# Retention slabs split from the unsplit tile, and the window groups' sample rows computed in the retention stage

## The chip, the cores and the metric

One core of one Trainium2 chip runs the kernel. The metric is the device time of one execution in microseconds (us); lower is better. A run is repeated and the median is given. The engines are TensorE (PE, with PEld for its weight loads), VectorE (DVE), ScalarE (ACT), GpSimd (POOL) and SyncE (SP), which here issues nearly all transfers (DMAs).

## The reference

One layer of a hybrid decoder for 1024 prompt tokens and 8 sample tokens (one token each of 8 requests), all in float32, model width 1024:

```
h = rms_norm(x) * g
[ret q|k|v|gate, swa q|k|v|gate, merge gates] = h @ w_in
A: retention, 4 heads (q, k of 128, v of 256), chunks of 128 tokens, state kept; sample rows: one step on a given state
B: sliding-window attention (128), 4 groups of 4 query heads and one key/value head of 64, sinks, rotary;
   sample rows: one query each against a cache of 128 rows, whose last row is the new key/value
y = x + (sigmoid(mr) * (gated A @ w_ret) + sigmoid(ms) * (gated B @ w_swa)) @ w_out
```

The outputs are y of prompt and samples, the retention states and the window caches.

## The kernel before, in words

A float32 operand is held as two parts, hi (rounded to PE's faster float32 form) and lo (the rest), and each product is three matmuls: hi·hi, hi·lo and lo·hi. Weights come from memory in *units*. A unit is loaded by SP into a raw tile `wraw` (3 buffers), ACT writes its hi part `whi` (L167) and POOL its lo part `wlo` (L168); 6 buffers of each. A T unit is 128 columns of w_in over all 8 blocks of 128 rows and feeds `gemm_T` (L211 to L213): 24 matmuls for one block of 344 of the 1032 tokens. A K unit (*slab*) is 2 of the 8 row blocks of a group's 384 columns; four slabs feed `gemm_tok` (L221 to L223): 24 matmuls for one tile of 128 tokens.

The first phase begins with the startup: 9 token tiles x0 to x8 (x8 holds the 8 sample rows) are loaded, normed (`norm_h`; DVE's product is L281, its 1/root comes from POOL, L146), transposed on PE (L286) and split into `hhi` and `hlo` (L138, L139). For x8 two more forms are stored: `hx`, its plain float32 transposed, and `hs`, with the hi rows at columns 0 to 7 and the lo rows at 32 to 39 of 40 (L290, L292). Then come four retention groups (gi 0 to 3, one head each) and four window groups (gi 4 to 7). A group works through 8 token tiles; between them stand T blocks: gates, merge gates, and the retention q, whose rotation is three operations on DVE (L325 to L327).

The sample rows of a group are computed apart. In a retention group `quad_rows` (L249) takes the *unsplit* weights: the group's 384 columns are loaded a second time, whole, into `rraw` (L241), and 8 matmuls with the 8 columns of `hx` go to four column tiles of PE; one ACT copy and three DVE additions (L250, L252) sum the four. In a window group `gemm_rows` (L231, L232) takes the split weights that the group has anyway: 16 matmuls of `hs` with `whi` and `wlo`, an ACT copy (L235) and a DVE addition (L236). Then the rows get their rotation, the new key is stored in the cache tile `cK`, which POOL copies to `kc` (L617) for PE's transposes (L620).

A second phase does the branch projections and the output. The program is put in order by the framework's scheduler (L1029), which decides what stands before what on every engine, so a change in one place can move instructions in another. SP and each engine take their list in order: an instruction that waits holds up what stands behind it.

Of the kernel before, what the change touches and what calls it, by code (L numbers as in the profile page):

```python
# [9 lines left out]
F32 = mybir.dt.float32  # L10
F32R = mybir.dt.float32r
# [7 lines left out]
P = 128  # L19
# [26 lines left out]

MROW = 40
MLO = 32
KST = 64 + NS
# [7 lines left out]
QAT = (1, 2, 4)  # L57
ROW = [2, 0, 0, 0, 2, 0, 0, 1]
FILL = [3, 2, 2, 2, 9, 9, 9, 4]
# [62 lines left out]
class Body:  # L122
# [27 lines left out]
    def load_unit(self, spec):  # L150
        nc = self.nc
        kind, segs, k0, nk = spec
        width = sum(w for _, _, w in segs)
        raw = self.t(self.wp, [P, D], "wraw", bufs=RAW)
        hi = self.t(self.wp, [P, D], "whi", F32R, bufs=self.wbufs)
# [69 lines left out]

    def gemm_rows(self, ps, units, st, out, n):
        nc = self.nc
        k = 0
        for whi, wlo in units:
            for kk in range(whi.shape[1]):  # L230
                nc.tensor.matmul(ps, st[:, k, :], whi[:, kk, :], start=(k == 0), stop=False)  # L231
                nc.tensor.matmul(ps, st[:, k, :], wlo[:, kk, :], start=False, stop=(k == KT - 1))  # L232
                k += 1
        tmp = self.t(self.sm, [NS, 512], "rowtmp", bufs=1)
        nc.scalar.activation(out=tmp[:, :n], in_=ps[MLO : MLO + NS, :n], func=AF.Copy)  # L235
        nc.vector.tensor_tensor(out=out, in0=ps[:NS, :n], in1=tmp[:, :n], op=ALU.add)  # L236

    def load_rows(self, tile, segs):
# [16 lines left out]
    def norm_h(self, t):  # L255
# [26 lines left out]
        for half in range(2):  # L282
            ps = self.t(self.ptr, [P, 4, P], "tr")
            for j in range(4):
                k = half * 4 + j
                nc.tensor.transpose(out=ps[:, j, :p], in_=x[:p, k * P : (k + 1) * P], identity=self.ident[:p, :p])  # L286
            ks = slice(half * 4, half * 4 + 4)
            self.copy_hi_lo(self.hhi[:, ks, cs], self.hlo[:, ks, cs], ps[:, :, :p], nc.vector)
            if t == NT:
                nc.scalar.activation(out=self.hs[:, ks, 0:NS], in_=ps[:, :, :p], func=AF.Copy)  # L290
                nc.vector.tensor_copy(out=self.hx[:, ks, :], in_=ps[:, :, :p])
                nc.vector.tensor_copy(out=self.hs[:, ks, MLO : MLO + NS], in_=self.hlo[:, ks, cs].bitcast(F32))  # L292

# [297 lines left out]
    def swa_rows(self, g, units, oT):  # L591
        nc = self.nc
        gs = slice(g * HD, (g + 1) * HD)
        K, V = self.cK[:, :, gs], self.cV[:, :, gs]
        acc = self.t(self.pacc, [P, 512], "acc")
        kv = self.t(self.ap, [NS, 384], "rkv", bufs=1)
        self.gemm_rows(acc[:MROW, :384], units, self.hs, kv[:], 384)
        qr, kd, rs = self.swa_rope(kv[:], NT, NS)
# [78 lines left out]
    def build(self):  # L677
# [4 lines left out]
        with tc.tile_pool(name="const", bufs=1, reuse_waits="tile") as cp, tc.tile_pool(name="sm", bufs=2, reuse_waits="tile") as sm, \  # L682
# [6 lines left out]
            self.d_o = [self.t(dp, [P, TOK], f"d_o{k}") for k in range(16)]  # L689
            self.d_t = [self.t(dp, [P, TOK], f"d_t{k}") for k in range(16)]  # L690
            self.d_m = [self.t(dp, [P, TOK], f"d_m{k}") for k in range(8)]
            self.misc = self.t(cp, [P, NMISC], "misc")
# [9 lines left out]
    def phase1(self):  # L702
        nc, tc = self.nc, self.tc
        with tc.tile_pool(name="h", bufs=1, reuse_waits="tile") as hp:
            self.hhi = self.t(hp, [P, KT, TOK], "hhi", F32R)
            self.hlo = self.t(hp, [P, KT, TOK], "hlo", F32R)
            self.hs = self.t(hp, [P, KT, MROW], "hs", F32R)
            self.hx = self.t(hp, [P, KT, NS], "hx")
            nc.vector.memset(self.hs[:].bitcast(F32), 0.0)
            self.hT = [(self.hhi[:, k, :], self.hlo[:, k, :]) for k in range(KT)]  # L710
# [6 lines left out]
    def groups(self):  # L717
        nc = self.nc
        tch = lambda c: ("T", (("w_in", c, P),), 0, KT)

        def slabs(cols):
            return [("K", tuple(("w_in", c, w) for c, w in cols), 2 * j, 2) for j in range(4)]

# [26 lines left out]

        kv = slabs([(OFF_RK, DK), (OFF_RV, DV)])
        qu = tch(OFF_RQ)
# [27 lines left out]
        def tables(us):  # L780
# [6 lines left out]
        steps += [([], begin, 0), x(0), w(kv[0]), x(1), w(kv[1]), x(2), w(kv[2]), w(kv[3]), ([], tables, 0), x(3), w(qu),  # L787
                  x(4), x(5), rope_block(0), x(6), x(7), x(8), rope_block(1), rope_block(2)]
        prev = []
        pipe = []  # L790
# [5 lines left out]
        for gi in range(8):  # L796
# [5 lines left out]
            if ret:  # L802
                h = gi

                def setup(us, h=h, st=st):
                    st["o"] = self.t(self.gp, [P, 2, TOK], "oT", bufs=2)
                    st["q"] = self.t(self.ap, [P, TOK], "qT", bufs=2)
                    st["S"] = self.t(self.ap, [P, DV], "S", bufs=2)
                    self.rraw = self.t(self.ap, [P, KT, 384], "rraw", bufs=1)
                    self.load_rows(self.rraw, [("w_in", OFF_RK + h * DK, DK), ("w_in", OFF_RV + h * DV, DV)])  # L810
                put(([], setup))
                qs = [([tch(OFF_RQ + h * DK)], lambda us, st=st, nb=nb: self.ret_q(us[0], st["q"], nb)) for nb in range(NB)]
                if h:
                    put(*qs)
                kv = slabs([(OFF_RK + h * DK, DK), (OFF_RV + h * DV, DV)])
                mk = lambda u, t, h=h, st=st: self.ret_tile(h, t, u, st["q"], st, st["o"])
                mkr = lambda u, h=h, st=st: self.ret_rows(h, u, st["q"], st["o"])
            else:
# [7 lines left out]
                put(([], setup))  # L826
                kv = slabs([(OFF_SQ + g * G * HD, G * HD), (OFF_SK + g * HD, HD), (OFF_SV + g * HD, HD)])
                mk = lambda u, t, g=g, st=st: self.swa_tile(g, t, u, st, st["o"])
# [6 lines left out]
            for t in range(NT + extra):  # L835
# [14 lines left out]
                p2 = pipe[-2] if len(pipe) > 1 else None  # L850
                p3 = pipe[-3] if len(pipe) > 2 else None
                if ret:
                    put(p1, p2, p3, *f, p1)
                else:
                    put(p1, p2, p1, *f[:1])
                    put(p2, *f[1:])
# [176 lines left out]
```

## Time and profile before

| | |
|---|---|
| median of 3 runs | 1169.08 us (1168.95 to 1169.35) |
| the profiled execution's own time | 1167.54 us |
| its span, first to last instruction | 1165.8 us |
| PE busy | 1142.7 us, 98% of the span |
| DVE, ACT, POOL busy | 644.0, 437.4, 427.5 us |
| mean granted clock of PE | 0.996 |
| moved by DMA | 126.99 MB |

The span is what the trace shows of one execution; its own time has 1.7 us around the span, and the median of the runs is 1.5 us above the profiled one. The share of busy time is a mean: PE has nearly all of its idle time in the first 50 us, where the token tiles arrive. A granted clock of 1 is 2.4 GHz, one of 0.5 is 1.2 GHz.

### The profile page before, as it was taken

What the parts mean: (1) busy time and instruction counts of PE and PEld (TensorE: products, weight loads), DVE (VectorE), ACT (ScalarE), POOL (GpSimd) and SP (SyncE); (2) the same over time, 40 slices, a digit from 0 to 9 for tenths busy, and PEclk for the clock granted to TensorE, in tenths of its full rate; (3) what the DMA queues carried; (4) which work ended last, traced back from release to release, by engine and by line L of the source; (5) the groups of instructions that cost most, each with busy time, mean ns of one, the idle gap of its engine ahead of it and who ended that gap; (6) DMA issues with size and microseconds to landing.
All of it is one profiled execution on the core that took longest, in us unless ns stands there. A gap on an engine that the chain in (4) does not pass through costs nothing.

```text
span 1165.8 us, 19287 instructions
## 1 busy us (share of the span) xinstructions
PE 1142.7 (98%) x7140; PEld 1088.8 (93%) x7140; DVE 644.0 (55%) x1823; ACT 437.4 (38%) x1130; POOL 427.5 (37%) x398
## 2 busy tenths in 40 slices
PE   6899999999999999999999999999999999999998
PEld 5899999999999999999999999999999999999876
DVE  5664645655644487767765776577744411665131
ACT  5444343334344244544463445345544210221010
POOL 4425116316225434634463446235751221221010
PEclk9899999999999999999999999999999999999999
DMA  9434315413123412311141114102437754546431
GB/s 319 124 111 130 115 43 165 154 60 100 47 81 104 141 32 59 91 60 31 34 133 44 33 33 139 38 1 64 151 115 249 230 152 130 179 139 206 158 101 64
DMA packets 135565, 126.99 MB, mean 109 GB/s; under 512 B 17768, under 2 KB 121576, under 8 KB 135440
## 3 DMA queue, kind: packets, MB, share of 16 engines
q1 hardware_dynamic: 128560, 117.32, 32.2%
q10 hardware_dynamic: 6912, 8.46, 2.0%
q8 instruction: 56, 0.92, 0.3%
q14 instruction: 37, 0.30, 0.1%
HBM read 95.37 MB, written 32.44 MB: 110 GB/s over the span
## 4 chain that ended last, share of the span: by engine, by line
PE 90%; DVE 4%; DMA 2%; issue 1%; ACT 1%; POOL 1%; SPq 0%; ACTq 0%; POOLq 0%
PE acc L211 16%; PE acc L212 16%; PE acc L213 15%; PE acc L221 10%; PE acc L223 10%; PE acc L222 10%; PE sc L550 1%; PE sc L551 1%; DMA oT<-in_x_prompt 1%; PE av L583 1%; PE av L582 1%; PE tr L562 1%; DMA oT<-d_o 1%; PE acc L249 1%; PE sc L201 1%
## 5 line engine op out<-in xcount | busy, mean ns | idle before, releaser
L168 POOL TENSOR_TENSOR wlo<-wraw,whi 128x1024 fp32r<-128x1024 f32 (+1 forms) x92 | 205.9, 2245 | 292.3 <-ACT whi L167 291.6
L211 PE MATMUL acc<-hhi,whi 128*128 128x344 f32 x864 | 279.5, 323 | 3.6 <-DVE rng L885 2.5
L212 PE MATMUL acc<-hlo,whi 128*128 128x344 f32 x864 | 277.8, 322 | 0.0
L213 PE MATMUL acc<-hhi,wlo 128*128 128x344 f32 x864 | 276.9, 321 | 0.0
L221 PE MATMUL acc<-whi,hhi 128*128 128x384 f32 x512 | 176.8, 346 | 2.3 <-DVE tg L302 1.2
L222 PE MATMUL acc<-wlo,hhi 128*128 128x384 f32 x512 | 176.1, 344 | 0.0
L223 PE MATMUL acc<-whi,hlo 128*128 128x384 f32 x512 | 175.8, 343 | 0.0
L211 PEld LDWEIGHTS acc<-hhi,whi 128*128 128x128 f32 x864 | 162.4, 188 | 6.1 <-ACT whi L167 2.7
L212 PEld LDWEIGHTS acc<-hlo,whi 128*128 128x128 f32 x864 | 162.4, 188 | 1.7 <-issue 0.4
L213 PEld LDWEIGHTS acc<-hhi,wlo 128*128 128x128 f32 x864 | 162.4, 188 | 1.0
L167 ACT ACTIVATE whi<-wraw 128x1024 fp32r<-128x1024 f32 (+1 forms) x92 | 90.3, 984 | 166.6 <-PE acc L212 110.4
L146 POOL TENSOR_TENSOR rs<-ms,nhalf 128x1 f32<-128x1 f32 (+3 forms) x81 | 68.6, 848 | 229.0 <-DVE ms L145 226.5
L221 PEld LDWEIGHTS acc<-whi,hhi 128*128 128x128 f32 x512 | 97.8, 191 | 5.1 <-issue 1.4
L223 PEld LDWEIGHTS acc<-whi,hlo 128*128 128x128 f32 x512 | 97.9, 191 | 0.9 <-issue 0.4
L222 PEld LDWEIGHTS acc<-wlo,hhi 128*128 128x128 f32 x512 | 98.0, 191 | 0.6 <-issue 0.2
L304 POOL TENSOR_TENSOR oT<-oT,tg 128x344 f32<-128x344 f32 x48 | 48.3, 1007 | 63.1 <-DVE tg L302 52.4
L504 ACT ACTIVATE s<-sc,ng,rs 128x128 f32<-128x128 f32 x128 | 56.9, 455 | 23.1 <-DVE ng L501 22.8
L223 PE MATMUL acc<-whi,mlo 128*128 128x512 f32 x128 | 50.5, 395 | 0.0
L221 PE MATMUL acc<-whi,mhi 128*128 128x512 f32 x128 | 50.4, 394 | 0.0
L222 PE MATMUL acc<-wlo,mhi 128*128 128x512 f32 x128 | 50.3, 393 | 0.0
L1000 DVE TENSOR_TENSOR x<-acc,x 128x512 f32<-128x512 f32 x16 | 11.1, 692 | 71.0 <-PE acc L223 71.0
L302 DVE SCALAR_TENSOR_TENSOR tg<-tg,acc 128x344 f32<-128x344 f32 x48 | 24.5, 510 | 31.8 <-ACT tg L301 31.6
(363 smaller groups left out, 2343.0 us busy)
## 6 DMA issues: line engine op xcount, KB each, us to landing
wraw<-in_w_in SPq DMA_DIRECT2D x36, 512.0 KB
d_t<-tg ACTq DMA_DIRECT2D x48, 172.0 KB
d_o<-oT SPq DMA_DIRECT2D x16, 516.0 KB
tt<-d_t SPq DMA_DIRECT2D x48, 172.0 KB
wraw<-in_w_in SPq DMA_DIRECT2D x32, 256.0 KB
st<-d_o SPq DMA_DIRECT2D x9, 516.0 KB
d_m<-tt SPq DMA_DIRECT2D x24, 172.0 KB
mm<-d_m SPq DMA_DIRECT2D x24, 172.0 KB
```

Of the source, the lines that this page charges most:

```text
L146: nc.gpsimd.tensor_tensor(out=rs[:p, :width], in0=ms[:p, :width], in1=self.nhalf[:p, :width], op=ALU.pow)
L167: nc.scalar.activation(out=hi[:, :f], in_=raw[:, :f], func=AF.Copy)
L168: nc.gpsimd.tensor_tensor(out=lo[:, :f], in0=raw[:, :f], in1=hi[:, :f].bitcast(F32), op=ALU.subtract)
L211: nc.tensor.matmul(ps, whi[:, k, :], hi[:, cs], start=(k == 0), stop=False)
L212: nc.tensor.matmul(ps, whi[:, k, :], lo[:, cs], start=False, stop=False)
L213: nc.tensor.matmul(ps, wlo[:, k, :], hi[:, cs], start=False, stop=(k == KT - 1))
L221: nc.tensor.matmul(ps, hi[:, k, a:b], whi[:, kk, :], start=(k == 0), stop=False)
L222: nc.tensor.matmul(ps, hi[:, k, a:b], wlo[:, kk, :], start=False, stop=False)
L223: nc.tensor.matmul(ps, lo[:, k, a:b], whi[:, kk, :], start=False, stop=(k == KT - 1))
L302: nc.vector.scalar_tensor_tensor(out=tg[:], in0=tg[:], scalar=1.0, in1=ps[:, :BL], op0=ALU.add, op1=ALU.mult)
L304: nc.gpsimd.tensor_tensor(out=sl, in0=sl, in1=tg[:], op=ALU.mult)
L504: nc.scalar.activation(out=s[:p, j, :], in_=src[j], func=AF.Exp, bias=ng[:p, j : j + 1], scale=scale[j], accum_out=l[:p, j : j + 1])
```

## The change

1. A retention group's slabs (now of kind "R") are loaded into slices of one `rraw` tile (one buffer), and ACT and POOL split them from there. `quad_rows` of the group reads the same tile. The second load of the columns goes.
2. In each retention group gi, later in its token loop, `fetch_rows` loads the 384 q, k and v columns of window group gi, unsplit, into `rraw`, and `window_rows` computes the sample rows of that window group with `quad_rows` and stores them in a small tensor `d_kv[g]` in memory.
3. In a window group the rows are loaded from `d_kv[g]`; `gemm_rows`, the tile `hs`, its memset and its four copies go.
4. The rows of the first window group begin one token tile earlier (ROW).

The bytes of weights moved stay the same: four loads of 1.5 MB go and four of 1.5 MB come.

```diff
-ROW = [2, 0, 0, 0, 2, 0, 0, 1]
+ROW = [2, 0, 0, 0, 1, 0, 0, 1]
...
-        raw = self.t(self.wp, [P, D], "wraw", bufs=RAW)
+        if kind == "R":
+            if k0 == 0:
+                self.rraw = self.t(self.ap, [P, KT, width], "rraw", bufs=1)
+            raw = self.rraw[:, k0 : k0 + nk, :].rearrange("p k c -> p (k c)")
+        else:
+            raw = self.t(self.wp, [P, D], "wraw", bufs=RAW)
...
-    def gemm_rows(self, ps, units, st, out, n):
...
             if t == NT:
-                nc.scalar.activation(out=self.hs[:, ks, 0:NS], in_=ps[:, :, :p], func=AF.Copy)
                 nc.vector.tensor_copy(out=self.hx[:, ks, :], in_=ps[:, :, :p])
-                nc.vector.tensor_copy(out=self.hs[:, ks, MLO : MLO + NS], in_=self.hlo[:, ks, cs].bitcast(F32))
...
-        acc = self.t(self.pacc, [P, 512], "acc")
         kv = self.t(self.ap, [NS, 384], "rkv", bufs=1)
-        self.gemm_rows(acc[:MROW, :384], units, self.hs, kv[:], 384)
+        nc.sync.dma_start(out=kv[:], in_=self.d_kv[g])
+        yield
...
+        window_cols = lambda g: [(OFF_SQ + g * G * HD, G * HD), (OFF_SK + g * HD, HD), (OFF_SV + g * HD, HD)]
+
+        def fetch_rows(g):
+            def fn(us):
+                self.rraw = self.t(self.ap, [P, KT, 384], "rraw", bufs=1)
+                self.load_rows(self.rraw, [("w_in", c, w) for c, w in window_cols(g)])
+            return ([], fn)
+
+        def window_rows(g):
+            def fn(us):
+                acc = self.t(self.pacc, [P, 512], "acc")
+                kv = self.t(self.ap, [NS, 384], "wkv", bufs=1)
+                self.quad_rows(acc, self.hx, self.rraw, kv[:], 384)
+                nc.sync.dma_start(out=self.d_kv[g], in_=kv[:])
+            return ([], fn)
...
-                    self.rraw = self.t(self.ap, [P, KT, 384], "rraw", bufs=1)
-                    self.load_rows(self.rraw, [("w_in", OFF_RK + h * DK, DK), ("w_in", OFF_RV + h * DV, DV)])
...
-                kv = slabs([(OFF_RK + h * DK, DK), (OFF_RV + h * DV, DV)])
+                kv = slabs([(OFF_RK + h * DK, DK), (OFF_RV + h * DV, DV)], "R")
...
+                if ret and t == (4 if gi == 0 else 2):
+                    put(fetch_rows(gi))
+                if ret and t == (6 if gi == 0 else 5):
+                    put(window_rows(gi))
```

The order of the instructions moves with it, at three places. The line numbers of the changed kernel are lower by 9 to 11 (L249 is L240, L211 is L214, L221 is L224, L146 is L144, L168 is L171).

The first is PE in the window stage, first window group, where the sample rows of that group stood, between a token tile's matmuls and a T block. Before:

```order
L223 MATMUL acc_5086<-whi_4838,hlo_122 128x384
L529 MATMUL tr_4987<-ident_63,qr_4890 128x128 x2
L231 MATMUL acc_5136<-whi_4500,hs_123 40x384
L232 MATMUL acc_5136<-wlo_4501,hs_123 40x384
L231 MATMUL acc_5136<-whi_4500,hs_123 40x384
L232 MATMUL acc_5136<-wlo_4501,hs_123 40x384
...
L529 MATMUL tr_5188<-ident_63,qr_4968 128x128 x2
```

and after:

```order
L226 MATMUL acc_5138<-whi_4888,hlo_126 128x384
L518 MATMUL tr_5039<-ident_63,qr_4940 128x128 x2
L214 MATMUL acc_5270<-hhi_125,whi_4902 128x344
L215 MATMUL acc_5270<-hlo_126,whi_4902 128x344
L216 MATMUL acc_5270<-hhi_125,wlo_4903 128x344
```

The 16 matmuls of `hs` are gone (four times in all, 64 matmuls), and the next T block stands in their place; apart from that the window stage has the same matmuls, in an order that differs in places.

The second is PE in the second retention group, where the sample rows of a window group come in. Before (`tr` of `on` and `kr` are transposes of a retention tile):

```order
L223 MATMUL acc_1975<-whi_1406,hlo_122 128x384
L211 MATMUL acc_2046<-hhi_121,whi_1419 128x344
L212 MATMUL acc_2046<-hlo_122,whi_1419 128x344
L355 MATMUL tr_2015<-ident_63,on_1927 128x128 x2
L381 MATMUL tr_2020<-ident_63,kr_1898 128x128
L213 MATMUL acc_2046<-hhi_121,wlo_1420 128x344
```

and after:

```order
L226 MATMUL acc_1984<-whi_1411,hlo_126 128x384
L240 MATMUL acc_2029<-rraw_1710,hx_127 8x384
L344 MATMUL tr_2024<-ident_63,on_1936 128x128 x2
L240 MATMUL acc_2029<-rraw_1710,hx_127 8x384 x7
L370 MATMUL tr_2044<-ident_63,kr_1907 128x128
L214 MATMUL acc_2070<-hhi_125,whi_1424 128x344
```

Eight quad matmuls are added, cut in two pieces by a transpose; it is the same in the third and fourth retention group, and in the first there are three pieces (2, 4 and 2).

The third is the startup: SP's list from x3 (`oT_211`) to x8, and a stretch of POOL's. SP before:

```order
L266 DMA oT_211<-in_x_prompt 128x1024
L266 DMA qT_279<-in_x_prompt 128x1024
L769 DMA ropeT_141<-in_c_ropeT 128x2x344 x2
...
L241 DMA rraw_412<-in_w_in 128x8x128
L241 DMA rraw_412<-in_w_in 128x8x256
L161 DMA wraw_273<-in_w_in 128x8x128
L884 DMA rng_111<-in_ret_norm_g 128x8x1
L266 DMA oT_302<-in_x_prompt 128x1024 x2
L161 DMA wraw_403<-in_w_in 128x8x128
L266 DMA oT_349<-in_x_prompt 128x1024
L266 DMA oT_349<-in_x_sample 8x1024
```

and after:

```order
L257 DMA oT_212<-in_x_prompt 128x1024
L164 DMA wraw_272<-in_w_in 128x8x128
L257 DMA qT_278<-in_x_prompt 128x1024
L757 DMA ropeT_143<-in_c_ropeT 128x2x344 x3
L164 DMA wraw_398<-in_w_in 128x8x128
L164 DMA wraw_845<-in_w_in 128x8x128
L890 DMA rng_115<-in_ret_norm_g 128x8x1
L257 DMA oT_301<-in_x_prompt 128x1024 x2
L164 DMA wraw_1417<-in_w_in 128x8x128
L257 DMA oT_348<-in_x_prompt 128x1024
L257 DMA oT_348<-in_x_sample 8x1024
```

The two `rraw` loads (1.5 MB) no longer stand ahead of x5 to x8; two more T units of 0.5 MB do. POOL before:

```order
L278 TENSOR_TENSOR oT_302<-oT_302,st_152 128x1024
L146 TENSOR_TENSOR rs_330<-ms_329,nhalf_68 128x1
L168 TENSOR_TENSOR wlo_405<-wraw_403,whi_404 128x1024
L146 TENSOR_TENSOR rs_354<-ms_353,nhalf_68 128x1
L146 TENSOR_TENSOR rs_377<-ms_376,nhalf_68 8x1
```

and after:

```order
L171 TENSOR_TENSOR wlo_400<-wraw_398,whi_399 128x1024
L317 TENSOR_TENSOR qT_405<-qT_405,ropeu_512 128x344
L144 TENSOR_TENSOR rs_306<-ms_305,nhalf_68 128x1
L269 TENSOR_TENSOR oT_301<-oT_301,st_154 128x1024
L137 TENSOR_TENSOR qlo_644<-qT_405,qhi_643 128x128
L144 TENSOR_TENSOR rs_329<-ms_328,nhalf_68 128x1
L144 TENSOR_TENSOR rs_353<-ms_352,nhalf_68 128x1
L144 TENSOR_TENSOR rs_376<-ms_375,nhalf_68 8x1
```

The T unit's split (`wlo` of 128x1024) stood ahead of the 1/root of x7 and x8 (`rs_354`, `rs_377`); now it stands ahead of that of x5 (`rs_306`). On DVE the first q rotation moves with it, from behind the norm of x8 to ahead of that of x5.

## Rows read from the trace of the kernel before

**Rows 1.** Page, part 1: busy us, share of the span, instructions, by engine

```profile
PE 1142.7 (98%) x7140; PEld 1088.8 (93%) x7140; DVE 644.0 (55%) x1823; ACT 437.4 (38%) x1130; POOL 427.5 (37%) x398
```

**Rows 2.** Waits of PE, 0 to 60 us: releaser, us in total, times, longest

```profile
PE tr L286 <- DVE oT L281: 8.1, 1, 8.1
PE acc L211 <- DVE rng L885: 2.5, 1, 2.5
PE tr L286 <- DVE hlo L139: 2.3, 3, 1.5
...
PE tr L381 <- DVE hs L292: 0.7, 1, 0.7
```

**Rows 3.** Windows: length, then busy us (x instructions) by engine, clock, DMA

```profile
core 0: us, PE busy (x) PEld busy (x) DVE busy (x) ACT busy (x) POOL busy (x), PEclk, DMA share, GB/s
...
28.00:32.00 4.00, 2.06 (x9) 2.06 (x10) 2.09 (x9) 3.72 (x8) 2.03 (x1) 0.87 1.05 359
32.00:36.00 4.00, 4.00 (x18) 4.00 (x18) 3.10 (x1) 2.97 (x6) 3.23 (x3) 0.71 1.13 318
...
40.00:50.00 10.00, 7.52 (x53) 6.55 (x51) 9.52 (x19) 3.52 (x10) 3.19 (x5) 1.00 0.37 93
...
60.00:350.00 290.00, 290.00 (x1913) 278.35 (x1912) 156.91 (x497) 114.96 (x317) 96.99 (x101) 1.00 0.31 100
...
350.00:905.00 555.00, 550.58 (x3525) 533.05 (x3525) 362.34 (x1116) 254.10 (x704) 263.87 (x251) 1.00 0.27 82
```

**Rows 4.** Chain of waits, 0 to 60 us: start, us, what

```profile
27.43 7.11 DMA oT<-in_x_prompt
...
37.04 2.39 POOL wlo L168
...
43.04 0.43 DVE qT L325
...
44.55 1.29 DVE hlo L139 x2
...
49.65 0.13 DVE hs L292
...
50.10 0.76 PE acc L249 x8
...
55.63 0.76 PE acc L249 x8
```

**Rows 5.** Line L231, and PE's timeline over the last group's sample rows

```profile
L231 PE MATMUL acc<-whi,hs x32: 332/338/420, 409.3 to 747.5; 128*40 128x384 f32 x32
...
745.08 0.33 PE L231 MATMUL acc<-whi,hs 128*40 128x384 f32 x1
...
747.89 0.38 PE L529 MATMUL tr<-ident,qr 128*128 128x128 f32 x2
```

**Rows 6.** PE's timeline over one quad in the retention stage

```profile
303.07 0.34 PE L223 MATMUL acc<-whi,hlo 128*128 128x384 f32 x1
303.34 1.48 PE L249 MATMUL acc<-rraw,hx 128*8 128x384 f32 x16
304.75 0.33 PE L381 MATMUL tr<-ident,kr 128*128 128x128 f32 x1
```

**Rows 7.** Lines L235 and L252: ns min/median/max, first and last start

```profile
L235 ACT ACTIVATE rowtmp<-acc x4: 481/482/482, 412.5 to 749.4; 8x384 f32<-8x384 f32 x4
...
L252 DVE TENSOR_TENSOR rkv<-acc,rkv x12: 549/552/559, 57.2 to 307.1; 8x384 f32<-8x384 f32 x12
```

**Rows 8.** Timeline: PE at 80.69 and 113.53, POOL at 96.21

```profile
80.69 0.27 PE L381 MATMUL tr<-ident,kr 128*128 128x128 f32 x1
...
96.21 1.85 POOL L168 TENSOR_TENSOR wlo<-wraw,whi 128x768 fp32r<-128x768 f32 x1 [0.62 <-ACT whi L167]
...
113.53 0.34 PE L221 MATMUL acc<-whi,hhi 128*128 128x384 f32 x1
```

**Rows 9.** Timeline, first window group's keys: POOL at 421.54, PE at 433.79

```profile
421.54 0.61 POOL L617 COPY kc<-cK 128x512 f32<-128x512 f32 x1 [2.00 <-DMA cK<-kd]
...
433.79 0.60 PE L620 MATMUL tr<-ident,kc 128*128 128x128 f32 x4
```

More of the change, by code (lines that the diff above doesn't have):

```diff
@@ L45 @@
 OFF_MS = OFF_MR + D
-MROW = 40
-MLO = 32
 KST = 64 + NS
@@ L224, in gemm_tok @@
                 k += 1
-    def gemm_rows(self, ps, units, st, out, n):
[L227 to L236, printed above, removed]
     def load_rows(self, tile, segs):
@@ L690, in build @@
             self.d_t = [self.t(dp, [P, TOK], f"d_t{k}") for k in range(16)]
+            self.d_kv = [self.t(dp, [NS, 384], f"d_kv{g}") for g in range(KVH)]
             self.d_m = [self.t(dp, [P, TOK], f"d_m{k}") for k in range(8)]
@@ L706, in phase1 @@
             self.hlo = self.t(hp, [P, KT, TOK], "hlo", F32R)
-            self.hs = self.t(hp, [P, KT, MROW], "hs", F32R)
             self.hx = self.t(hp, [P, KT, NS], "hx")
-            nc.vector.memset(self.hs[:].bitcast(F32), 0.0)
             self.hT = [(self.hhi[:, k, :], self.hlo[:, k, :]) for k in range(KT)]
@@ L719, in groups, with slabs @@
         tch = lambda c: ("T", (("w_in", c, P),), 0, KT)
-        def slabs(cols):
-            return [("K", tuple(("w_in", c, w) for c, w in cols), 2 * j, 2) for j in range(4)]
+        def slabs(cols, kind):
+            return [(kind, tuple(("w_in", c, w) for c, w in cols), 2 * j, 2) for j in range(4)]
         mg = [([tch(OFF_MR + c * P)], (lambda us, c=c, nb=nb: self.mg_block(us[0], c, nb))) for c in range(16) for nb in range(NB)]
@@ L749, in first @@
             return (us, fn), ([], more)
-        kv = slabs([(OFF_RK, DK), (OFF_RV, DV)])
+        kv = slabs([(OFF_RK, DK), (OFF_RV, DV)], "R")
         qu = tch(OFF_RQ)
@@ L826, in groups @@
                 put(([], setup))
-                kv = slabs([(OFF_SQ + g * G * HD, G * HD), (OFF_SK + g * HD, HD), (OFF_SV + g * HD, HD)])
+                kv = slabs(window_cols(g), "K")
                 mk = lambda u, t, g=g, st=st: self.swa_tile(g, t, u, st, st["o"])
```

## Prediction

> **What bounds the kernel now.** I read the busy times first: PE is busy 98% of the span, 1142.7 of 1165.8 us, and no other engine passes 55% [rows 1]. So time is won in two ways only: fewer or shorter matmuls, or less of PE's 23 us of idle time. The waits of PE say where that idle time lies: 8.1 us is the wait for the first tile, which the change does not touch; another 2.5 us stands before the first matmul of the q unit (27.5 to 29.9; the releaser named is a small DVE operation, but these weights were issued behind the `rraw` load), and 2.3 us and 0.7 us around the last transposes of the startup [rows 2]. The windows confirm it. From 60 to 350 us, the retention stage, PE is busy 290.00 of 290.00; from 350 to 905, the window stage and the fill behind it, 550.58 of 555.00; between 40 and 50 us it works 7.52 of 10 and DVE 9.52 [rows 3]. What is added in the retention stage therefore costs its full PE time, what is removed in the window stage gains its full PE time, and in the startup only the chain counts. That chain [rows 4] runs through the transfer of x7, which is issued at 27.43 and lands 7.11 later at 34.54; POOL's split of a T unit at 37.04, after which POOL makes x7's 1/root; and then DVE's operations in a row, up to the last copy into `hs` at 49.65, before PE goes on.
>
> **Part 1, the rows leave the window stage.** Each group loses 16 matmuls of `hs`. One is recorded with 0.33 to 0.34 us, but they overlap; the price is the pace: the group begins at 745.08 and the next instruction at 747.89, 2.81 us [rows 5]. Four groups: 4 × 2.81 = −11.2 us. PE waits 4.4 us in all of that stage, none of it on these matmuls, so nothing there hides the gain. The ACT copy (0.48 us each) and DVE addition removed with them [rows 7] lay beside PE.
>
> **Part 2, four more quads in the retention stage.** The same quad, of the same shape, stands there today, once in each group. The matmul before it starts at 303.07 and takes 0.18 at the pace of rows 5, the instruction after it starts at 304.75: 304.75 − 303.07 − 0.18 = 1.50 us [rows 6]. Four quads: +6.0 us. The bounds of one: 1.41 us from its own start to the next instruction; above, 16 records that don't overlap at all, at the pace of rows 5, 2.81 us, which would take the whole gain of part 1. I take 1.50, measured in that stage. The changed order cuts the new quads into two or three pieces. The quad of the startup is cut so today: 0.76 + 0.76 = 1.52 us [rows 4], so a cut costs some 0.02 us and I add nothing. Here a rule of the Trainium skill speaks against the change: the page "TensorEngine Tiling (Array Packing)", section Tiling Modes, Key Properties, says that a change of tiling mode (not just of the tile) drains TensorE, and each piece is such a change, there and back. The row shows 0.09 us between the end of the pace before the quad and its start, and this is inside the 1.50. By the rule, taken with 0.09 us for each of five extra cuts and for both directions, the sum would be 0.9 us worse; the cut quad that the trace has doesn't bear it out.
>
> The copy and three additions of each new quad (0.48 and 3 × 0.55 us) [rows 7] come to 1.65 us of DVE for each group, where DVE is busy 157 of 290 us [rows 3]: nothing. If that cover were gone, the accumulator of a later block would wait for them, at most 2.1 us for a group.
>
> **Part 3, one `rraw` for slabs and fetch.** The weights' bytes are the same. What is new is a chain: the slabs of the next group can be loaded only when PE has read the window columns out of the same buffer, and these only after the group's own rows. The new quad of the first group stands next to the transpose of `kr` which is at 80.69 today. The last slab of the second group is split at 96.21 now, taking 1.85 us, and first read by PE at 113.53 [rows 8]. From the quad to the first use are 32.8 us; four slabs need 1.5 MB (at 318 GB/s [rows 3], 5 us) and four splits of 1.85 us, 7.4: some 12 us if nothing overlaps. So 20 us of slack, cost nothing. Behind the waiting slab loads on SP stand the store of `d_kv` and the loads of the sample states; those have the next group's rows ahead of them.
>
> **Part 4, the window rows come by a load.** A group's rows are read from memory, 12 KB, written hundreds of us before. The later chain stays: POOL waits 2.00 us for the new key in `cK`, copies until 422.15, and PE transposes at 433.79, 11.6 us later [rows 9]. Starting one tile earlier makes that no worse. The window stage's other matmuls stand in a slightly different order; PE waits 4.4 us there now and I have no row that says whether this falls or rises. Bounds −4.4 and about +4; I take 0.
>
> **Part 5, the startup.** Three things move the chain. The transfers are the limit up to x7 (share of the queues 1.05 and 1.13 in 28 to 36 us [rows 3]), and ahead of x7 there is now 1.5 MB less of `rraw` and 1.0 MB more of T units: 0.52 MB at 318 GB/s is 1.6 us. POOL's 2.39 us split no longer stands before x7's 1/root. And one rotation on DVE, 43.04 to 44.55, 1.5 us [rows 4], goes ahead of x5. The last two are no clear gain: they are moved to where x5 and x6 need POOL and DVE, and DVE is busy 9.52 of 10 us at the end. The four copies into `hs` go for good: 2 × 0.13 us of DVE on the chain and about as much of ACT, 0.4. The end of the chain could be from 0 (another wait takes its place) to 1.6 + 2.4 + 1.5 + 0.4 = 5.9 us earlier; PE's waits there, 2.5 + 2.3 + 0.7, allow 5.5. I take the arrivals and the copies, 1.6 + 0.4 = −2.0 us, as the nearest to a row that I can show. Apart from it stands the clock. It is granted at 0.87 and 0.71 in the two windows after the wait of 2.5 us, which is a stretch at 1.2 in place of 2.4 GHz costing (0.13 + 0.29) × 4 = 1.7 us [rows 3]; one stretch more or less is worth that, and I count none.
>
> **Sum,** against the profiled execution's own 1167.54: −11.2 + 6.0 − 2.0 = −7.2, so 1160.3. The median of the runs is 1.5 us above the profiled time: **1161.9 us**.
>
> **Rivals.** (A) The startup gives nothing, since DVE, full at the end, is only handed its work in another order: −5.2, 1163.9 us. For it speaks DVE's 9.52 of 10; against it that DVE is idle nearly half of 28 to 32 us and can take the rotation there. (B) The startup's waits vanish with both stretches of low clock that follow them: −5.2 − 5.5 − 1.7 × 2 gives 1155.0. Against it: POOL and DVE have no less to do, bar the copies. (C) The gain is eaten: the new order in the window stage brings waits of 4 us, or the quads, cut up, cost 2.8 and not 1.5 (1169.08 − 2.0 = 1167.1). Three quads measured alike speak against the latter. This is "no change". (D) Slower, by one mechanism: the shared `rraw` buffer makes the slabs late. Its place is the first tile of the second to fourth retention groups, where PE has no wait today. The price is what the slabs come too late, three times; it eats the gain of 7.2 from 2.4 us for each group on, and to be slower by 0.2% takes 3.2. That the slack of 20 us would have to be gone first speaks against it; for it, that SP's list holds loads which wait for outputs ahead of these slabs in the third and fourth groups. At 5 us for each group: 1161.9 + 15 = 1177. That the change leaves matmuls as they were is excluded: 64 go and 32 come by the order.
>
> **How the numbers follow.** A measurement of this kernel tells about 0.2%, 2.3 us, from no change: faster is under 1166.7, slower over 1171.4. Forecast 0.46, A 0.27, B 0.10: faster, together 0.83. C 0.11: the same. D 0.06: slower. The likeliest case's own range, with 0 to 5.5 us in the startup left to A and B, is 1160 to 1163.5. The range of 8 in 10 goes down to half of the way from B, 1156, and up to where C begins, 1167.
>
> **What would show it.** In the changed profile: no matmul with 40 columns, eight quads of 16 records where there are four, each with 1.4 to 1.55 us from its start to the next instruction (both pieces together where it is cut); the retention stage longer by 6 us and without any wait of PE at a group's first tile (D would show one on `whi` or `wlo` there); the window stage shorter by 11 us with 3 to 6 us of waits (C: over 8); x7 landing at 33 us and PE's transpose after x8's at some 47.5 to 48 rather than 49.8 (A: 49 to 50; B: under 45 with the clock at 1.00 throughout). The forecast is wrong if a cut quad costs over 2 us, if `rraw` is waited for, or if a third stretch of low clock appears.

## The result and the profile after

| | before | after |
|---|---|---|
| median of 4 runs each | 1169.21 us (1168.95 to 1170.94) | 1177.83 us (1177.03 to 1178.51) |
| ratio, 95% interval | | 1.007 (1.0053 to 1.0088) |
| the profiled execution, its span | 1167.54, 1165.8 us | 1178.24, 1176.3 us |
| mean granted clock of PE | 0.996 | 0.993 |

The changed kernel is slower by 8.6 us; forecast were 7 us less. Engine by engine (page, part 1) the answer to [rows 1] is:

```profile
PE 1148.0 (98%) x7140; PEld 1086.5 (92%) x7140; DVE 660.1 (56%) x1828; ACT 435.5 (37%) x1128; POOL 429.5 (37%) x398
```

PE has as many recorded instructions as before and is busy 5.3 us longer, over a span that grew by 10.5. Its waits in the whole run (releaser, us in total, times, longest) answer to [rows 2]:

```profile
PE tr L277 <- DVE oT L272: 8.1, 1, 8.1
PE tr L277 <- DVE ms L143: 3.1, 1, 3.1
PE tr L277 <- DVE hlo L137: 2.4, 2, 2.0
PE tr L551 <- DVE s L497: 1.9, 1, 1.9
PE acc L214 <- DVE tg L291: 1.9, 1, 1.9
PE tr L551 <- DVE oT L640: 1.3, 1, 1.3
...
PE sc L540 <- DVE kTlo L137: 0.8, 1, 0.8
```

The windows after, to be held beside [rows 3] with the same columns:

```profile
28.00:32.00 4.00, 4.00 (x28) 3.95 (x28) 3.92 (x8) 1.93 (x5) 1.95 (x1) 1.00 1.07 361
32.00:36.00 4.00, 2.31 (x14) 2.00 (x12) 3.19 (x4) 3.29 (x7) 3.58 (x3) 1.00 0.72 178
36.00:40.00 4.00, 2.49 (x9) 1.86 (x9) 3.39 (x7) 1.83 (x5) 3.12 (x5) 0.55 0.00 0
40.00:50.00 10.00, 8.16 (x39) 7.83 (x39) 4.84 (x8) 3.41 (x5) 0.00 (x0) 0.67 0.17 54
...
60.00:350.00 290.00, 290.00 (x1908) 271.87 (x1908) 165.87 (x495) 113.21 (x310) 93.74 (x96) 1.00 0.35 104
350.00:915.00 565.00, 556.71 (x3546) 538.73 (x3545) 372.39 (x1133) 255.20 (x716) 265.67 (x255) 1.00 0.26 80
```

Three things are to be seen. In the startup the wait of 2.5 us before the q unit is gone (PE 4.00 of 4.00 from 28 to 32 us), but one of 3.1 us stands at 34.3 us, and the clock is low in the next two windows. In the retention stage PE still never waits. From 350 us on its idle time has risen from 4.4 to 8.3 us, and there is a stretch of low clock that the kernel before doesn't have:

```profile
830.00:836.00 6.00, 5.49 (x25) 5.25 (x26) 4.54 (x19) 2.78 (x11) 3.22 (x4) 0.72 1.15 322
```

Two marks that both traces have split the 10.7 us between the profiled executions. They are PE's first transpose of `kr` behind x8's rows, and the transposes of `qr` that stood ahead of the first group's sample rows [rows 5]. PE's timeline (start, us, what), before and then after:

```profile
49.80 0.30 PE L381 MATMUL tr<-ident,kr 128*128 128x128 f32 x1 [0.70 <-DVE hs L292]
...
409.12 0.38 PE L529 MATMUL tr<-ident,qr 128*128 128x128 f32 x2
```

```profile
52.35 0.30 PE L370 MATMUL tr<-ident,kr 128*128 128x128 f32 x1 [0.17 <-DVE hx L281]
...
422.74 0.38 PE L518 MATMUL tr<-ident,qr 128*128 128x128 f32 x2
```

Startup +2.6 (forecast −2.0); retention stage 13.62 − 2.55 = +11.1 (forecast +6.0); what lies behind 10.7 − 13.6 = −2.9 (forecast −11.2).

### The profile page after: what moved, and what is told of

It is laid out like the page before. It is cut to its first block, busy times and chain, and to the rows that moved or that the text cites. A ratio compares the mean times of both kernels' runs of the same rounds, so it can differ in the third digit from the quotient of the medians.

```text
span 1176.3 us, 19304 instructions
## 1 busy us (share of the span) xinstructions
PE 1148.0 (98%) x7140; PEld 1086.5 (92%) x7140; DVE 660.1 (56%) x1828; ACT 435.5 (37%) x1128; POOL 429.5 (37%) x398
## 5 line engine op out<-in xcount | busy, mean ns | idle before, releaser
L214 PE MATMUL acc<-hhi,whi 128*128 128x344 f32 x864 | 282.4, 327 | 2.6 <-DVE tg L291 1.9
L171 POOL TENSOR_TENSOR wlo<-wraw,whi 128x1024 fp32r<-128x1024 f32 (+1 forms) x76 | 175.5, 2316 | 270.5 <-ACT whi L170 246.0
L224 PE MATMUL acc<-whi,hhi 128*128 128x384 f32 x512 | 175.5, 343 | 2.5 <-DVE tg L291 1.2
L214 PEld LDWEIGHTS acc<-hhi,whi 128*128 128x128 f32 x864 | 163.9, 190 | 4.8 <-DVE tg L291 2.2
L144 POOL TENSOR_TENSOR rs<-ms,nhalf 128x1 f32<-128x1 f32 (+3 forms) x81 | 68.9, 853 | 227.0 <-DVE ms L143 212.2
L170 ACT ACTIVATE whi<-wraw 128x1024 fp32r<-128x1024 f32 (+1 forms) x76 | 76.5, 1012 | 128.4 <-PE acc L215 84.5
L224 PEld LDWEIGHTS acc<-whi,hhi 128*128 128x128 f32 x512 | 97.2, 190 | 5.0 <-ACT hhi L136 1.5
L1006 DVE TENSOR_TENSOR x<-acc,x 128x512 f32<-128x512 f32 x16 | 11.1, 692 | 71.0 <-PE acc L226 71.0
L224 PE MATMUL acc<-whi,mhi 128*128 128x512 f32 x128 | 50.4, 394 | 0.0
```

The lines of the kernel that those rows point to most:

```text
L144: nc.gpsimd.tensor_tensor(out=rs[:p, :width], in0=ms[:p, :width], in1=self.nhalf[:p, :width], op=ALU.pow)
L170: nc.scalar.activation(out=hi[:, :f], in_=raw[:, :f], func=AF.Copy)
L171: nc.gpsimd.tensor_tensor(out=lo[:, :f], in0=raw[:, :f], in1=hi[:, :f].bitcast(F32), op=ALU.subtract)
L214: nc.tensor.matmul(ps, whi[:, k, :], hi[:, cs], start=(k == 0), stop=False)
L224: nc.tensor.matmul(ps, hi[:, k, a:b], whi[:, kk, :], start=(k == 0), stop=False)
```

## The experiments

All were timed in five rounds, each against runs of the kernel before on its own chip (medians 1169.08 to 1169.40). "Startup", "retention" and "window and end" are differences of a profiled execution from that of before up to the first mark, between the two, and behind the second. They are of one execution each and carry its scatter: slabs_same_order below has the window stage of the kernel before, and its profiled execution, 3.4 us above its median, is 4.3 us longer there. The medians are the firmer numbers.

**The slabs and the startup.** The first kernel does part 1 of the change alone, on the kernel before:

```
-        raw = self.t(self.wp, [P, D], "wraw", bufs=RAW)
+        if kind == "R":
+            if k0 == 0:
+                self.rraw = self.t(self.ap, [P, KT, width], "rraw", bufs=1)
+            raw = self.rraw[:, k0 : k0 + nk, :].rearrange("p k c -> p (k c)")
...
-                    self.rraw = self.t(self.ap, [P, KT, 384], "rraw", bufs=1)
-                    self.load_rows(self.rraw, [("w_in", OFF_RK + h * DK, DK), ("w_in", OFF_RV + h * DV, DV)])
```

> The kernel before with only the first part of the change: slabs in the one buffer, no second load, the window groups' rows left in the window stage. Its PE order differs from that of before in the startup alone. Theory: the startup loses what it loses in the changed kernel, 2.6 us up to the first quad, 1169.2 to 1171.8, give or take one stretch of low clock (1.7). Rival: the shared buffer is the whole cause, 1177 or more. My forecast's term (the startup gains 2.0) would give 1167.2.

1171.67 us, ratio 1.002 (1.001 to 1.0029). Startup +3.0, retention 0.0, window and end +1.6. So sharing the buffer costs the retention stage nothing, and the startup's loss belongs to this part. The next one is the changed kernel with four T loads queued on SP behind x8's rows:

```
+HELD = (5, 6, 7, 8)
...
+                if len(loaded) in HELD:
+                    with self.tc.issue_after(self.xload.ins):
+                        loaded.append(self.load_unit(units[len(loaded)]))
```

> The changed kernel with the loads of four T units queued on SP behind that of x8, so that 1.5 MB less stands ahead of x5 to x8; PE's order in the startup differs by six instructions. If the transfers set the end of the startup: some 3 to 5 us earlier, 1173 to 1175. If the chain of DVE and POOL does (x5's norm beside POOL's product for x6, 3.36 us): at most 0.7 us, the wait for x7's landing, 1177.

1178.51 us, 1.0082 (1.0068 to 1.0096), startup +2.5 as after. The norm of x5 starts at 29.11 us here and at 33.90 after, and the startup ends no earlier: PE now waits 4.4 us behind x7's norm, which takes 3.86 us beside POOL's work. So earlier token tiles alone don't shorten the startup.

From here on some kernels have a fixed order: a table gives each engine's list and SP's, taken from the kernel before for all instructions that both have, and each instruction is tied behind the one ahead of it on the same engine, where it takes its turn anyway. Nothing waits for another engine by it.

```
+    for name, order in table.items():
+        mine = [i for i in traced if i.engine == kinds[name]]
+        for a, b in zip(order, order[1:]):
+            tc.add_manual_dep(
+                mine[b], mine[a].name, mybir.DependencyInfo(mybir.DependencyClass.NoSync, mybir.DependencyReason.DATA), reason="in_order"
+            )
```

The edit of slabs_only in the order of before:

> slabs_only in the order of the kernel before (PE, DVE and the matched instructions of ACT, POOL and SP). Theory (the 2.6 us of the startup are lost by the new order): as before within one stretch of low clock, 1169 to 1171. If the second load was worth something, as the forecast had it: 1167. Rival (the one buffer itself costs): 1171.7 as slabs_only, with waits on the slabs.

1170.19 us, 1.0006 (0.9998 to 1.0014): no different from before. The second load of 1.5 MB was worth nothing when it went, and what slabs_only lost (2.3 us by the medians, 3.0 in the startup of its trace) was the scheduler's new order.

**The quads.** In the changed kernel they are cut. PE's timeline of the second and third retention group (start, us, line, shape, records; each matmul has two records):

```profile
165.26 0.81 PE L240 MATMUL acc<-rraw,hx 128*8 128x384 f32 x2
166.00 0.44 PE L344 MATMUL tr<-ident,on 128*128 128x128 f32 x2
166.37 1.47 PE L240 MATMUL acc<-rraw,hx 128*8 128x384 f32 x14
167.77 0.33 PE L370 MATMUL tr<-ident,kr 128*128 128x128 f32 x1
...
219.38 1.48 PE L240 MATMUL acc<-rraw,hx 128*8 128x384 f32 x16
220.79 0.33 PE L370 MATMUL tr<-ident,kr 128*128 128x128 f32 x1
```

A single matmul takes 166.00 − 165.26 = 0.74 us to the next instruction, the other seven 1.40, all eight together 1.41. The startup's cut quad [rows 4] had 0.76 for four. So a piece costs a whole pass over the four column tiles, however few of them it fills. The retention stage's own quad in the startup, cut four and four before, is cut in three now, 4 + 1 + 3; its second and third piece:

```profile
57.57 0.81 PE L240 MATMUL acc<-rraw,hx 128*8 128x384 f32 x2
58.31 0.49 PE L380 MATMUL av<-qT,kT 128*128 128x128 f32 x2
...
59.09 0.82 PE L240 MATMUL acc<-rraw,hx 128*8 128x384 f32 x6
59.84 0.33 PE L370 MATMUL tr<-ident,kr 128*128 128x128 f32 x1
```

Three matmuls take 59.84 − 59.09 = 0.75 us, and that is one pass more than before. To undo the cuts of the added quads, these are traced behind the last 60 matmuls ahead of them, and the tile's next steps behind the quad:

```
+                    for i in [i for i in nc.cur_bb.bb.instructions if i.engine == nc.tensor.engine][-60:]:
+                        stack.enter_context(self.tc.issue_after(i))
                     self.quad_rows(acc, self.hx, self.rraw, kv[:], 384)
```

> The changed kernel with the eight matmuls of each window quad kept together (queued on PE behind what was written before them); nothing else moves except some T blocks in the first retention group. Theory (three separate costs, one of them the cut quads): in the changed kernel a quad cut behind its first matmul takes 0.74 + 1.40 us, a whole one 1.41, and the first group's, cut 2+4+2, takes 2.26; whole ones save 3 x 0.8 + 0.9 = 3.4 us, 1177.8 to 1174.4. Rival (one cause, the shared buffer: slabs and fetches wait for each other): the cuts are without effect, 1177.8.

1179.7 us, 1.0096 (1.0079 to 1.0113), outside both expectations. In groups 2 to 4 the quads are whole, at 1.41, and from group to group the interval between the old quads falls from 95.2 to 94.30 us (before: 92.74), so 1.56 instead of 2.46 for one. But the new order in the first group brought waits of 1.9 us between 70 and 120 us and a stretch of 6.8 us at clock 0.5. The same, but with the slabs in their own buffers again and the second load back:

```
-        if kind == "R":
-            if k0 == 0:
-                self.rraw = self.t(self.ap, [P, KT, width], "rraw", bufs=1)
-            raw = self.rraw[:, k0 : k0 + nk, :].rearrange("p k c -> p (k c)")
-        else:
-            raw = self.t(self.wp, [P, D], "wraw", bufs=RAW)
+        raw = self.t(self.wp, [P, D], "wraw", bufs=RAW)
...
+                    self.rraw = self.t(self.ap, [P, KT, 384], "rraw", bufs=1)
+                    self.load_rows(self.rraw, [("w_in", OFF_RK + h * DK, DK), ("w_in", OFF_RV + h * DV, DV)])
```

> The other part alone: startup, slabs and second load as before, the window groups' rows in the retention stage with whole quads, four more loads of 1.5 MB. Theory: -11.4 for the matmuls of hs, +6.0 for four whole quads at 1.50, and the window stage keeps the waits that it has in the changed kernel, some +7: 1170.8. Rival (the shared buffer is the cause, and it is not shared between slabs and fetches here): 1169.2 - 5.4 = 1163.8.

1175.98 us, 1.0056 (1.0042 to 1.0069), 5 us above the expectation. Startup −0.6, retention +10.0, of which 6.2 are quads (the rest is in the first group, where PE waits 1.4 us at 82 us and the low clock lasts longer); window and end only −1.1. With the startup out of the way and the slabs in their own buffers, the window stage still gives hardly any of its 11 us.

**The window stage.** The kernel before without the 64 `hs` matmuls and with nothing in their stead; the rows' numbers are read from the input:

```
-        self.gemm_rows(acc[:MROW, :384], units, self.hs, kv[:], 384)
+        nc.sync.dma_start(out=kv[:], in_=self.i["x_sample"][:, 0, g * HD : g * HD + 384])
```

> The kernel before without the 64 matmuls of hs; the window groups' sample rows are read from the sample input instead, so their values are not the reference's; no quad is added. It measures the gain of the first term alone. If order costs nothing, 1169.2 - 11.4 = 1157.8. If the window stage without them waits as it does in the changed kernel (some 7 us more than before), 1164.8.

1169.23 us, 0.9996 (0.9986 to 1.0006). 11.4 us of PE's work are gone (before, the four groups' matmuls took 2.99, 2.79, 2.80 and 2.81 us to the next instruction) and not one is gained. Behind the second mark PE waits 10.7 us where it waited 2.7: 4.4 at the turn to the second phase, 2.9 at 813 us, 1.8 at 784 to 786 and 1.3 at 490, and two stretches of low clock, which cost 1.7 us each, come on top. The two longest waits are for ACT (`tg` and `qs`), and ahead of the longest ACT itself waits 5.2 us for a load. Next the changed kernel with that kernel's window order (no tile's pause ahead of the rows' rotation, ROW as before):

```
-ROW = [2, 0, 0, 0, 1, 0, 0, 1]
+ROW = [2, 0, 0, 0, 2, 0, 0, 1]
...
-        yield
```

> The changed kernel with the rows of the window groups begun as in the kernel before (first group at its third tile, no pause behind the load), which makes the scheduler's order of the window stage that of no_hs_rows; startup and retention stage as in the changed kernel. Theory (the order decides): the window stage and the end cost what they cost in no_hs_rows, 4 us more than in the changed kernel by the two profiles: 1182. Rival (the chain decides, the order doesn't): 1177.8 as the changed kernel.

1177.68 us, 1.0079 (1.0066 to 1.0092): as after, as the rival said; window and end −3.8. This one point of the order doesn't decide it. So no_hs_rows again, now in the order of before:

> As no_hs_rows (the window groups' rows read from the sample input, values not the reference's), but every engine and SP keeps the order that it has in the kernel before; only the 64 matmuls, their copies and additions are missing. Theory (the gain of the first term is lost to the new order that the scheduler makes of the window stage): 1169.3 - 11.4 = 1157.9. Rival (another engine's chain sets the pace of the window stage, so PE time that goes there becomes idle time in any order): 1165 to 1169, with waits of PE on DVE or ACT of 7 us or more.

1165.16 us, 0.997 (0.9955 to 0.9984), at the lower end of the rival's range. Held beside before, instruction by instruction, each group's rows give 2.7 to 2.8 us at their place; then 1.9 are lost by 426 us, 0.6 each at 510 and 624, 2.0 at 786 to 788 and 1.5 by low clock behind it. The first of these places shows why. Windows, before and then here:

```profile
409.00:425.00 16.00, 16.00 (x103) 15.05 (x102) 14.05 (x45) 7.32 (x22) 6.29 (x5) 1.00 0.01 2
```

```profile
409.00:425.00 16.00, 14.22 (x92) 13.90 (x91) 13.83 (x44) 5.54 (x15) 6.34 (x6) 1.00 0.01 1
```

PE has less to do, DVE has as much as before and is busy 13.83 of 16 us. The timeline at the end of the stretch, before:

```profile
422.20 0.16 DVE L501 SCALAR_TENSOR_TENSOR ng<-mx,nsink 128x4 f32<-128x4 f32 x1
...
422.20 2.43 POOL L168 TENSOR_TENSOR wlo<-wraw,whi 128x1024 fp32r<-128x1024 f32 x1
...
422.39 2.25 DVE L502 TENSOR_TENSOR ds<-sink,ng 128x4 f32<-128x4 f32 x1
424.57 0.50 DVE L302 SCALAR_TENSOR_TENSOR tg<-tg,acc 128x344 f32<-128x344 f32 x1
```

and in no_hs_same_order:

```profile
421.77 2.37 POOL L171 TENSOR_TENSOR wlo<-wraw,whi 128x1024 fp32r<-128x1024 f32 x1
...
421.86 2.30 DVE L504 SCALAR_TENSOR_TENSOR ng<-mx,nsink 128x4 f32<-128x4 f32 x1
424.19 0.16 DVE L505 TENSOR_TENSOR ds<-sink,ng 128x4 f32<-128x4 f32 x1
424.27 0.51 DVE L305 SCALAR_TENSOR_TENSOR tg<-tg,acc 128x344 f32<-128x344 f32 x1
...
424.84 0.44 PE L224 MATMUL acc<-whi,hhi 128*128 128x384 f32 x1 [1.78 <-DVE tg L305]
```

The product `tg` that empties PE's accumulator starts at 424.57 before and at 424.27 here. DVE has come 0.3 us forward, PE 2.7 us, and PE waits for the rest. In both kernels 2.1 us of DVE's busy time here is one small operation (`ds` or `ng`, 0.16 us elsewhere) that stands beside POOL's split of a unit. Now the whole change, in the order of before, each added quad whole behind the last matmul of its token tile:

> The whole change, but every instruction that both kernels have stands in the order of the kernel before (startup and window stage included), and each window quad stands whole behind the last matmul of its token tile. Theory: the gain of no_hs_same_order, less four whole quads at 1.56 us, less about 0.4 for the copies into hs: 1169.3 - 11.4 + 6.2 - 0.4 = 1163.7. Rival (the pace of the window stage is set elsewhere): 1171 or more. Rival (the shared buffer makes slabs late): waits of PE on whi or wlo at a group's first tile.

1171.91 us, 1.0026 (1.0016 to 1.0036): 5.9 us under the changed kernel, by order and whole quads alone, and still slower than before, as the first rival said. Startup +0.3, retention +7.5 (6.4 are quads; the low clock behind the first mark lasts longer, which is worth 1.3), window and end −4.6. The wait of 2.5 us before the q unit is still there, though no `rraw` load stands ahead of those weights. In both kernels the weight load in front of it waits 2.7 us for ACT's split of them, which ACT begins here at 29.13 us behind `khi` without a pause, so no transfer holds it. The same with each added quad cut behind its first matmul; only the table differs. PE's list at the second group's quad:

```
 L229 MATMUL acc<-whi,hlo 128x384
-L243 MATMUL acc<-rraw,hx 8x384 x8
+L243 MATMUL acc<-rraw,hx 8x384
 L217 MATMUL acc<-hhi,whi 128x344
 L218 MATMUL acc<-hlo,whi 128x344
+L243 MATMUL acc<-rraw,hx 8x384 x7
 L347 MATMUL tr<-ident,on 128x128 x2
```

> full_same_order with one thing changed: each of the four window quads is cut behind its first matmul by the two PE instructions that follow. Theory (a piece costs a whole pass of four column tiles, 0.74 us, however few matmuls it holds): three passes and not two, some 0.85 us for each quad, 3.4 in all: 1171.9 to 1175.3. Rival (the forecast's reading, a cut costs 0.02 us): 1172.

1176.02 us, 1.0055 (1.0039 to 1.0071): 4.1 us above full_same_order, though its six runs reach from 1172.8 to 1179.1. The trace gives the size more closely: from one old quad to the next it is 95.22 us, and 94.34 in full_same_order, so a cut costs 0.88 us and four cost 3.5. If DVE sets the pace, taking DVE's work away must give the rest. full_same_order without the norm and rotation of the sample q and k, 15 DVE operations less in each window group (and an ACT square and a 1/root on POOL); the rows are used unrotated:

```
-        qr, kd, rs = self.swa_rope(kv[:], NT, NS)
-        nc.sync.dma_start(out=K[0:1], in_=kd[:NS, 0, :])
+        nc.sync.dma_start(out=K[0:1], in_=kv[:, 256:320])
```

> full_same_order without the norm and rotation of the window groups' sample q and k (the rows are used as they come, values not the reference's): 14 DVE operations fewer for each group, some 4.5 us of DVE in the stretch behind the rows, no PE instruction less. Theory (DVE sets the pace there, so PE's gain becomes waits for DVE): the waits of 1.9, 0.6 and 0.6 us behind the first three groups' rows go, 1171.9 to 1169 or less. Rival (the waits come from the order or from PE's own sequence): 1171.9.

1164.1 us, 0.9959 (0.9946 to 0.9972). 7.8 us for some 60 small DVE operations; window and end −11.4, just what the 64 matmuls took. PE's waits behind the second mark are 2.7 us, as before the change, where full_same_order has 7.9; instruction by instruction 1.8 us come back behind the first group's rows, 0.7, 0.7 and 2.1 behind the others, and 1.0 at the turn to the second phase. Behind the first group's rows:

```profile
426.47 0.16 DVE L493 SCALAR_TENSOR_TENSOR ng<-mx,nsink 128x4 f32<-128x4 f32 x1
...
427.36 2.40 POOL L174 TENSOR_TENSOR wlo<-wraw,whi 128x1024 fp32r<-128x1024 f32 x1 [2.40 <-ACT whi L173]
...
427.65 0.51 DVE L294 SCALAR_TENSOR_TENSOR tg<-tg,acc 128x344 f32<-128x344 f32 x1 [0.83 <-ACT tg L293]
```

and in full_same_order:

```profile
429.55 2.30 DVE L493 SCALAR_TENSOR_TENSOR ng<-mx,nsink 128x4 f32<-128x4 f32 x1
...
431.96 0.52 DVE L294 SCALAR_TENSOR_TENSOR tg<-tg,acc 128x344 f32<-128x344 f32 x1
...
432.53 0.45 PE L227 MATMUL acc<-whi,hhi 128*128 128x384 f32 x1 [1.79 <-DVE tg L294]
```

`tg` is 4.3 us earlier. So the edit frees DVE in two ways: its own operations go, and `ng` is through before POOL's split begins, which saves 2.1 us here and 2.2 at the fourth group's rows. That DVE was late is shown by this; which of the two parts freed PE was not told apart.

**A version that is faster.** The norm and rotation can be done in the retention stage, where DVE has room, behind each added quad, with tables of 8 rows (7 DVE operations for a group):

```
                 self.quad_rows(acc, self.hx, self.rraw, kv[:], 384)
+                rotate_rows(kv)
```

> full_same_order with nothing left out: the norm and rotation of the window groups' sample q and k are done in the retention stage, behind each window quad (two tables of 8 rows, 7 DVE operations for each group instead of 15, one ACT square, one 1/root on POOL), and the finished rows are stored in d_kv. Theory (what the window stage lacks is DVE time, and the retention stage has it): as rows_prepared, 1164.1, up to 1166, faster than the kernel before. Rival (the 4.5 us of DVE for each group come back as waits in the retention stage): 1169 or more, with waits of PE between 80 and 360 us.

**1165.5 us**, 0.9971 (0.996 to 0.9981): below both kernels, with nothing left out. Window and end −10.1, retention +7.7 with one new wait of 1.0 us, startup +0.7. The same place of the program, in full_same_order and then here (windows, columns as above):

```profile
417.00:433.00 16.00, 14.21 (x92) 13.93 (x91) 13.60 (x42) 5.86 (x17) 6.65 (x6) 1.00 0.02 3
```

```profile
417.00:433.00 16.00, 16.00 (x105) 15.96 (x104) 11.07 (x40) 6.80 (x22) 5.98 (x5) 1.00 0.11 31
```

DVE falls from 13.60 to 11.07 and PE rises to 16.00 of 16. The last kernel is the same edit in the order that the scheduler gives it:

> The same edit of the changed kernel, in the order that the scheduler itself makes, with quads cut as it likes. Theory (DVE relief plus three losses of order that stay: startup 2.6, cut quads 3.4, window order about 2): 1164.1 + 8 = 1172, and 5 or more below the changed kernel's 1177.8. Rival (the scheduler's order eats the relief): 1177.

1178.29 us, 1.0077 (1.0063 to 1.0092), as the rival said. The same instructions in two orders, one with whole and one with cut quads, are 12.8 us apart. Startup +3.3, retention +11.05, window and end −3.4 with new waits for DVE (3.4 us for `s`) and ACT (3.7 us for `tg`) and two stretches of low clock behind them.

## Why the prediction was wrong, step by step

Between the forecast −7.2 and the +10.7 of the profiled executions lie 17.9 us: 8.3 behind the second mark (parts 1 and 4), 5.1 in the retention stage (part 2) and 4.6 in the startup (part 5).

**Part 1** failed at "none of it on these matmuls, so nothing there hides the gain". The 64 matmuls went and were worth 11.4 us of PE. But a wait that isn't there before can arise: DVE, at 14.05 of 16 us behind the first group's rows, was level with PE, and PE only ran ahead into it. In an unchanged order the net gain was 4.0 us (no_hs_same_order), in the scheduler's nothing (no_hs_rows). That it was DVE in the unchanged order is shown by rows_prepared, which gives the 7.8 us back; DVE's part in it is its own operations and its stand beside POOL's splits together. In the scheduler's order other waits come in their place, in no_hs_rows the longest for ACT. I read DVE as 362 us of 555, a mean, where the stretch behind each group's rows decides.

**Part 2**: the whole quad was right, 1.50 forecast, 1.56 to 1.60 measured. "A cut costs some 0.02 us" was wrong: a cut off the pass's edge costs a whole pass more, 0.74, and some 0.9 in all (0.88 in cut_same_order), and the cut of the startup, four and four, fell on the edge. In the trace of the changed kernel each added quad of groups 2 to 4 cost 2.4 to 2.5 us instead of 1.56, together 7.3. The first group is 3.8 us longer: its added quad, cut 2 + 4 + 2, has three passes, 2.26 us in place of 1.41, and the startup's own quad, now 4 + 1 + 3, has one more, 0.74. That is 1.56 + 0.85 + 0.74 = 3.2 by the passes; the other 0.6 wasn't placed. Of the 11.1 us four whole quads would be 6.2; the other 4.8 are nearly all cuts. The sign that a cut quad costs over 2 us did appear. The Trainium skill's rule on draining that stood there pointed the right way, but 0.09 us there and 0.09 back was a quarter of the price.

**Part 3** was right: no wait of PE at a group's first tile, and slabs_same_order is level with before. So rival D had the right sign of the change, not its mechanism.

**Part 4**: the waits behind the second mark rose by 3.9 us, inside −4.4 to +4 but at its end and not at 0; new ones of 5.9 us, all for DVE, stand at 502, 810, 826 and 828 us. What the bounds left out: a stretch of low clock at 832 us that costs 1.7, and some 3 us that no wait shows, spread over PE's matmuls in their new order. These, 8.5 us in all, are what −2.9 lacks to −11.4; the 3 us weren't traced further.

**Part 5**: −2.0 forecast, +2.6 measured. Both supports fell: arrivals don't set the end (loads_held) and the second load is worth nothing (slabs_same_order). x7's rows come no earlier (34.43 us, before 34.56), T loads took the place. What is late after is POOL and DVE work in another order. The timeline of the startup after:

```profile
27.55 2.40 POOL L171 TENSOR_TENSOR wlo<-wraw,whi 128x1024 fp32r<-128x1024 f32 x1 [2.76 <-ACT whi L170]
...
28.09 1.95 DVE L327 TENSOR_TENSOR kr<-kr,ku 128x64 f32<-128x64 f32 x1
...
33.83 2.35 POOL L269 TENSOR_TENSOR oT<-oT,st 128x1024 f32<-128x1024 f32 x1
...
33.90 3.36 DVE L272 SCALAR_TENSOR_TENSOR oT<-oT,rs,st 128x1024 f32<-128x1024 f32 x1 [0.78 <-POOL rs L144]
...
37.41 1.94 PE L277 MATMUL tr<-ident,oT 128*128 128x128 f32 x8 [3.10 <-DVE ms L143]
```

x5's norm waits for the 1/root, which POOL now does behind two other operations, and then takes 3.36 us beside POOL's own work, 2.1 more than another of its shape. PE stands 3.1 us, and the clock is at 0.5 from about 36.4 to 46.6 us. By the windows from 36 to 50 us that is (0.45 × 4 + 0.33 × 10) = 5.1 us of clock, where before the first mark the kernel before lost 1.7; the stretch of 1.7 behind the mark, between 50 and 60 us, is in both. How the +2.6 divides between the order's waits and the clock behind them was not told apart. The forecast's warning sign, a third stretch of low clock, did appear, at 832 us, and the first is three times as long as before.

**Rivals.** C had both real causes, waits in the window stage and dear cuts, but each as a small thing and with "no change" as its end; against the cuts I counted three whole quads, which say nothing of a cut. What no rival had is the order of the whole program.

**The sum again**, by the profiled executions. From the 1160.3 forecast to the 1170.7 of full_same_order are 10.4 us: 6.6 of part 1 (−4.6 where −11.2 was forecast), 1.5 in the retention stage (7.5 for 6.0, of it 1.3 of clock) and 2.3 in the startup (+0.3 for −2.0). From there to the changed kernel's 1178.2 are 7.5: 3.6 in the retention stage, which are those 4.8 less that clock, 2.2 in the startup and 1.7 behind it, what else the order moved. By the medians the two steps are 10.0 and 5.9.

## What to carry to other kernels

That PE is busy 98% does not make its removed work a gain: look at each other engine's busy time in the stretch right behind the removal (DVE had 85 to 88% here where the gain was lost, 69% where it came), and ask what the next instruction of PE waits for there. In a statically ordered program an edit moves instructions in places that it doesn't touch, so compare the edit under the old order first, and price the new order apart. A group of column-tiled matmuls like these should stay whole, or be cut only at a full pass. And where DVE is late, see what POOL does beside it: a small DVE operation of two inputs can take as long as POOL's.

## What the hardware showed that was not expected

- One matmul of a quad (8 columns by 384, float32, four column tiles) takes PE 0.74 us, three 0.75, four 0.76, seven 1.40, eight 1.41.
- A DVE operation on 128x4 took 2.25 and 2.30 us, with one of its own shape beside it at 0.16, where a POOL operation of two inputs and 2.4 us had started 0.1 to 0.2 us earlier; one on 128x64, begun 0.5 us behind a POOL split, took 1.95 (the one of the same shape and line before it 0.21). All three ended within 0.1 us of POOL's. The norm's 128x1024 product took 3.36 and ended 1.1 us behind POOL's 2.35; another of its shape took 1.28. The Trainium skill, page "GPSIMD Engine Reference", section 1. Specifications, says that GpSimd shares its SBUF interfaces with VectorE and that DVE instructions with two SBUF inputs contend with it. These rows agree and give the size: in them DVE stands until POOL is done, however small its own operation is. In rows_prepared `tg`, which has one of its two inputs in PE's accumulator, ran inside POOL's split (from 427.36 us) and took its usual 0.51.
- Around a wait of 3.1 us (34.3 to 37.4 us) the granted clock fell and stayed low for some 10 us (0.55 from 36 to 40 us, 0.67 from 40 to 50); before, behind the wait of 2.5 us, it was 0.87 and 0.71 in two windows of 4 us [rows 3].
